# Sparse attention's best keys: the first query block takes out its 16 least keys in two rounds, not its 112 best in 14

## The chip, the cores and the metric

The kernel runs on one core of a Trainium2 chip, in one launch. The metric is the device time in microseconds (us). The core has five engines that each work through their own instructions in the order of the program: TensorE (PE in the profile, with PEld for its weight loads), VectorE (DVE), ScalarE (ACT), GpSimd (POOL) and SyncE (SP), which here only starts transfers from memory. Work tiles have 128 partitions.

## The reference, cut to what matters

The program is a decoder trunk of two layers over 528 tokens (16 learned meta tokens, then 512 real ones), width 1024, in float32. Layer 0 is differential attention, layer 1 is sparse attention in which a small indexer picks the keys of each query; a gated feed-forward network (FFN) with a short convolution stands behind each. What is changed lies in the indexer of layer 1:

```python
topk = min(TOPK_MAX, n_keys // 4)            # 128
score = einsum('bqhk,bqh->bqk', relu(raw), wb)
causal = k_pos[None, :] <= q_pos[:, None]
score = where(causal & (k_pos < N_META)[None, :], BIG_SCORE, score)
score = where(causal, score, -inf)
top_val, top_idx = lax.top_k(score, topk)
valid = top_val > -inf
ks = gather(k, top_idx); vs = gather(v, top_idx)
s = where(valid, einsum(qb, ks), -inf)       # softmax over the picked keys
```

The 16 meta tokens are always among the 128 picked, so each query picks 112 of the others. Masked keys never count, whether picked or not.

## The kernel before

**Tiling.** Everything is held transposed, features on the partitions and tokens on the free axis. Queries are handled in one block of the 16 meta tokens (block 0) and four blocks of 128 (blocks 1 to 4, `BLK`, L38); block b sees 16 + 128 b keys. Block 1 therefore has 144 keys, 128 of them not meta.

**Arithmetic.** A float32 product is made of three rounded ones. `two` (L394) splits a tensor into a high part (a copy on ScalarE, `wh` for a weight slab of 128x1024) and a low part (a subtraction, `wl`), and `project` (L454) multiplies 48 times for each slab: high by high, high by low, low by high, over 8 pieces and two token spans. There are two pairs of `wh` and `wl`, so the next slab is split while one is in use.

**Layer 1.** `index_task` (L1070) gives eight passes of indexer scores that are summed into `acc[b]`, one tile for each block. `topk_task` (L1099) then marks the best keys of its block: 14 rounds, each of which finds the eight greatest values of the 128 rows (`max`) and overwrites them with `TAKEN` (`match_replace`, which the profile shows as a MATCH_VALUE_LOAD and a MATCH_REPLACE8). At the end a `tensor_scalar` turns marked places into 0 and all others into -1e30, a `tensor_tensor` lays the causal mask over it, GpSimd clears the meta columns, and `acc[b]` is the bias of all 16 heads. A head (L1186) may start once block 2's bias is there; its parts wait for their own block's (`e_bias`). Meanwhile PE works through the projections of q, k and v ("filler"). q and k of a pair of heads go through `rope` (multiply by `Cr`, shuffle, multiply by `Sr`, add), are split into `X` and `K` tiles (`q_stack`, `k_stack`), and each `K` is completed by a transfer from one half of its partitions to the other, issued by GpSimd. Only then can PE make the head's scores; the softmax is a fused subtract-and-minimum on VectorE (an ISA or CUSTOM_DVE instruction) and an exponential on ScalarE, and `probs_T` transposes and splits the result (`ph`, `pl`).

**What sets the order.** Nothing is ordered by hand. `Plan.run` (L292) holds all tasks and emits, again and again, the instruction that can start first by a table of costs (`_cost`, L71), with ties of up to 30 ns going to the task of higher priority. Work that VectorE or GpSimd could do alike stands in an `Alt` (L115), and the planner takes the engine on which it would end first, with a surcharge on VectorE (`plan.bias`). So when one instruction of a task goes or comes, the order behind it on all engines is drawn anew. The order, once drawn, is fixed in the program; at run time each engine waits for semaphores. All planned instructions have the line L272.

Of the kernel before, what the change touches and what calls it, by code (L numbers as in the profile page):

```python
# [13 lines left out]
ALU = mybir.AluOpType  # L14
# [6 lines left out]
NMETA = 16  # L21
# [7 lines left out]
NEG = -1e30  # L29
TAKEN = -3e38  # L30
TOPK = 128

BLK = [(0, 16)] + [(16 + 128 * i, 144 + 128 * i) for i in range(4)]
# [291 lines left out]
def hybrid_trunk(ctx: ExitStack, tc: tile.TileContext, A, out):  # L325
    nc = tc.nc
    plan = Plan(tc)
    v, s, g, pe, sy = (Engine(n, e) for n, e in (
        ("dve", nc.vector), ("act", nc.scalar), ("pool", nc.gpsimd), ("pe", nc.tensor), ("sp", nc.sync)))
# [8 lines left out]
    def bufs(name, n, shape, dtype=F32):  # L338
        return Buf([sb(f"{name}{i}", shape, dtype) for i in range(n)])
# [9 lines left out]
    TT = bufs("tt", 10, [P, T + 2])  # L349
# [642 lines left out]
    def attention1(norm, nxt):  # L992
# [106 lines left out]
        def topk_task(b):  # L1099
            yield e_acc[b]  # L1100
            st = yield STAT
            m8 = st[:, :8]
            w = acc[b][:, NMETA:]

            for _ in range((TOPK - NMETA) // 8):
                yield v.max(out=m8, in_=w)
                yield v.match_replace(out=w, in_to_replace=m8, in_values=w, imm_value=TAKEN)
            yield v.tensor_scalar(out=w, in0=w, scalar1=TAKEN, scalar2=NEG, op0=ALU.not_equal, op1=ALU.mult)
            if b == 4:
                plan.bias = SPARE_TAKEN  # L1110
            w = acc[b][:, BLK[b][0]:]
            yield v.tensor_tensor(out=w, in0=w, in1=mask[:, T - P:], op=ALU.min)
            yield g.memset(acc[b][:, :NMETA], 0.0)
            STAT.put(st)
            e_bias[b].set()
# [147 lines left out]
        for b in range(1, 5):  # L1263
            spawn(topk_task(b), 4)
# [193 lines left out]
```

## Time and profile before

| what | value |
|---|---|
| median of 3 runs | 1422.75 us (1421.95 to 1424.04) |
| the profiled execution, its own time | 1423.88 us |
| its span, first to last instruction | 1422.0 us |
| PE busy | 1367.0 us, 96% |
| VectorE busy | 953.3 us, 67% |
| ScalarE busy | 678.9 us, 48% |
| GpSimd busy | 333.7 us, 23% |
| VectorE, `max` and `match_replace` of all four blocks, first to last start | 744.1 to 804.3 us |
| granted clock of PE, mean | 0.989 |

A row of a timeline gives start, duration, engine, operation, and what was written from what (buffer numbers left out, so `acc` is any block's); in brackets the idle time before it and what ended it. A row of the windows gives for a stretch the busy time of each engine and its number of instructions, the share of full clock that PE was granted, and the load of the transfer engines. Durations of neighbours on VectorE overlap by some 0.06 us; from start to start counts.

### The profile page before, as it was taken

To read this page: it belongs to the slowest core of one execution; us is meant where nothing else is said; L and a number is where in the kernel's file an instruction comes from. 1 tells how busy PE (TensorE), PEld (TensorE's weight loads), DVE (VectorE), ACT (ScalarE), POOL (GpSimd) and SP (SyncE) were. 2 spreads that over 40 slices of the span, in tenths; PEclk is the share of its full clock that TensorE was granted. 3 is DMA by queue.
4 is the path that set the end of the run, shared out by engine and by line. 5 is a ranking of instruction groups with operands and counts; after the bars stand their busy time and mean duration, and the time that the engine had idled before them with its cause. 6 is when DMAs were issued, how large, how long until landed. Compare 5 with 4: busy or idle time off the path is not lost.

```text
span 1422.0 us, 26126 instructions
## 1 busy us (share of the span) xinstructions
PE 1367.0 (96%) x10662; PEld 1328.6 (93%) x10662; DVE 953.3 (67%) x1613; ACT 678.9 (48%) x1224; POOL 333.7 (23%) x432
## 2 busy tenths in 40 slices
PE   8899999999999999999989979999999999999997
PEld 7899998899999999999989879998999989989997
DVE  6976775457645754775699978887667637646764
ACT  5576665444423432443365376777444424423454
POOL 4645655420000000000347543332210000000012
PEclk9999999999999999999999989999999999999999
DMA  5323223223233223332212322232223232233333
GB/s 191 102 61 81 71 75 90 72 78 99 84 90 100 85 83 102 89 90 69 90 45 75 90 62 60 68 78 65 89 90 89 90 104 89 93 99 92 91 115 107
DMA packets 36519, 124.30 MB, mean 87 GB/s; under 512 B 4400, under 2 KB 4784, under 8 KB 36400
## 3 DMA queue, kind: packets, MB, share of 16 engines
q1 hardware_dynamic: 32544, 111.84, 25.9%
q0 software_dynamic: 2560, 8.65, 2.9%
q8 instruction: 84, 1.38, 0.4%
q10 hardware_dynamic: 1296, 2.15, 0.4%
q14 instruction: 35, 0.29, 0.1%
HBM read 111.88 MB, written 2.10 MB: 80 GB/s over the span
## 4 chain that ended last, share of the span: by engine, by line
PE 68%; DVE 10%; ACT 2%; issue 1%; POOL 0%; POOLq 0%; ACTq 0%; DVEq 0%
PE ps L272 68%; DVE tt L272 3%; DVE acc L272 3%; DVE st L272 2%; DVE wl L272 1%; DVE ns L272 1%; ACT ns L272 0%; ACT wh L272 0%; ACT tt L272 0%; DVE K L272 0%; POOL tt L272 0%; DVE pl L272 0%; ACT K L272 0%; DVE X L272 0%; ACT ph L272 0%
## 5 line engine op out<-in xcount | busy, mean ns | idle before, releaser
L272 PE MATMUL ps<-R,wh 128*128 128x256 f32 (+4 forms) x4000 | 679.4, 290 | 6.4 <-ACT wh L272 2.2
L272 PEld LDWEIGHTS ps<-R,wh 128*128 128x128 f32 (+1 forms) x4000 | 561.8, 190 | 15.2 <-ACT wh L272 2.4
L272 PE MATMUL ps<-R,K 128*128 128x272 f32 (+3 forms) x3264 | 430.6, 290 | 0.0
L272 PE MATMUL ps<-R,wl 128*128 128x272 f32 (+3 forms) x2000 | 423.1, 289 | 3.5 <-DVE wl L272 3.5
L272 PEld LDWEIGHTS ps<-R,K 128*128 128x128 f32 x3264 | 412.5, 189 | 8.4
L272 PEld LDWEIGHTS ps<-R,wl 128*128 128x128 f32 x2000 | 312.2, 189 | 7.3 <-DVE wl L272 4.4
L272 ACT CAST wh<-raw 128x1024 fp32r<-128x1024 f32 (+1 forms) x134 | 138.6, 1034 | 171.7 <-PE ps L272 127.0
L272 DVE TENSOR_TENSOR wl<-raw,wh 128x1024 fp32r<-128x1024 f32 (+1 forms) x124 | 156.5, 1262 | 23.1 <-ACT wh L272 21.7
L272 ACT CAST K<-raw 128x1024 fp32r<-128x1024 f32 (+1 forms) x77 | 79.1, 1027 | 140.0 <-PE ps L272 125.7
L272 DVE TENSOR_TENSOR h<-ps,h 128x528 f32<-128x528 f32 (+3 forms) x70 | 45.7, 653 | 143.1 <-PE ps L272 143.1
L272 POOL TENSOR_TENSOR acc<-acc,tt 128x528 f32<-128x528 f32 (+1 forms) x26 | 43.3, 1667 | 415.1 <-ACT tt L272 411.9
L272 DVE TENSOR_TENSOR tt<-ps,rbc 128x528 f32<-128x528 f32 (+2 forms) x89 | 62.4, 701 | 114.5 <-PE ps L272 110.1
L272 DVE SCALAR_TENSOR_TENSOR tt<-tt,cw,tt 128x528 f32<-128x528 f32 (+1 forms) x176 | 133.4, 758 | 8.2 <-ACT tt L272 4.9
L272 ACT CAST R<-tt 128x512 fp32r<-128x512 f32 (+2 forms) x84 | 48.7, 586 | 155.4 <-DVE tt L272 155.0
L272 DVE TENSOR_TENSOR K<-raw,K 128x1024 fp32r<-128x1024 f32 (+1 forms) x76 | 91.4, 1203 | 13.6 <-ACT K L272 12.3
L272 PE MATMUL ps<-K,X 128*128 128x272 f32 (+2 forms) x464 | 79.9, 308 | 13.2 <-DVE st L272 6.9
L272 ACT ACTIVATE ns<-ns,st 128x528 f32<-128x528 f32 (+4 forms) x160 | 82.1, 514 | 20.1 <-DVE st L272 17.1
L272 PEld LDWEIGHTS ps<-K,X 128*128 128x128 f32 x464 | 66.4, 184 | 18.0 <-DVE st L272 8.2
L272 ACT ACTIVATE tt<-tt,cw 128x528 f32<-128x528 f32 (+1 forms) x88 | 72.4, 822 | 14.6 <-DVE tt L272 14.5
L272 POOL MEMSET tt<- 128x2 f32 x44 | 4.2, 100 | 302.0 <-DVE tt L272 302.0
L272 POOL TENSOR_TENSOR tt<-tt,Sr 128x528 f32<-128x528 f32 x29 | 44.9, 1549 | 115.7 <-DVE tt L272 115.7
L272 ACT ACTIVATE tt<-tt 128x528 f32<-128x528 f32 (+1 forms) x44 | 28.1, 639 | 81.4 <-DVE tt L272 81.4
(112 smaller groups left out, 1315.5 us busy)
## 6 DMA issues: line engine op xcount, KB each, us to landing
raw<-in_ffn_up_dram SPq DMA_DIRECT2D x88, 512.0 KB, 3.6
raw<-in_ffn_down_dram SPq DMA_DIRECT2D x32, 448.0 KB, 3.3
raw<-in_da_qkv_dram SPq DMA_DIRECT2D x24, 512.0 KB, 3.7
raw<-in_dsa_qkv_dram SPq DMA_DIRECT2D x24, 512.0 KB, 3.6
raw<-in_ffn_down_dram SPq DMA_DIRECT2D x22, 512.0 KB, 3.6
K<-K POOLq DMA_DIRECT2D x32, 264.0 KB, 3.1
raw<-in_da_o_dram SPq DMA_DIRECT2D x8, 512.0 KB, 3.7
raw<-in_dsa_o_dram SPq DMA_DIRECT2D x8, 512.0 KB, 3.7
```

Source lines behind the costliest of these rows:

```text
L272: self.tc.keep_in_program_order(op.call(*op.a, **op.k))
```

## The change

Only `topk_task` is changed, and in it only what block 1 does, the one block with no more than `TOPK` (128) keys beside the meta ones. Instead of marking 112 of its 128 keys it marks the 16 others. ScalarE writes the negated scores, in reversed order, into a borrowed tile of the pool `TT`; two rounds of `max` and `match_replace` mark the 16 greatest of them, so the 16 least scores; and the `tensor_scalar` reads the tile backwards and gives the marked places -1e30 and the others 0. The reversal keeps the pick among equal scores as it was. Blocks 2, 3 and 4 keep their 14 rounds.

```diff
@@ topk_task
             w = acc[b][:, NMETA:]
-
-            for _ in range((TOPK - NMETA) // 8):
-                yield v.max(out=m8, in_=w)
-                yield v.match_replace(out=w, in_to_replace=m8, in_values=w, imm_value=TAKEN)
-            yield v.tensor_scalar(out=w, in0=w, scalar1=TAKEN, scalar2=NEG, op0=ALU.not_equal, op1=ALU.mult)
+            n = BLK[b][1] - NMETA
+            if n <= TOPK:
+                t = yield TT
+                u = t[:, :n]
+                yield s.mul(u, w[:, ::-1], -1.0)
+                for _ in range((n - (TOPK - NMETA)) // 8):
+                    yield v.max(out=m8, in_=u)
+                    yield v.match_replace(out=u, in_to_replace=m8, in_values=u, imm_value=TAKEN)
+                yield v.tensor_scalar(out=w, in0=u[:, ::-1], scalar1=TAKEN, scalar2=NEG, op0=ALU.is_equal, op1=ALU.mult)
+                TT.put(t)
+            else:
+                for _ in range((TOPK - NMETA) // 8):
+                    ...
```

The planner draws a new order from there to the end of layer 1's attention; the order in front of it and that of the second FFN are the same. Over the whole program VectorE has 32 rows fewer (24 of the rounds, and 8 net that go to GpSimd: 5 K splits, 4 X splits and 3 additions, against which 2 `wl` splits and 2 others come back), GpSimd 8 more, PE as many as before.

On VectorE, at the end of block 1's two rounds (`acc_142` is block 1's tile, `acc_143` block 2's, `tt_104` the borrowed one):

```order
+L272 TENSOR_SCALAR acc_142<-tt_104 128x128
 L272 MAX st_136<-acc_143 128x8
-L272 MAX st_135<-acc_142 128x8
+L272 TENSOR_TENSOR acc_142<-acc_142,mask 128x128
 L272 MATCH_REPLACE acc_143<-st_136,acc_143 128x256
-L272 MATCH_REPLACE acc_142<-st_135,acc_142 128x128
+L272 TENSOR_TENSOR wl_115<-raw_111,wh_114 128x1024
 L272 MAX st_136<-acc_143 128x8
-L272 MAX st_135<-acc_142 128x8
+L272 TENSOR_TENSOR tt_109<-tt_108,Cr 128x528
```

Block 1's rounds are gone from between those of block 2, and a weight split and the rotation of q stand in their place.

On GpSimd, at the same time of the program (`R_75`, `R_69` are parts of v; `X_118` and `K_123` belong to the first pair of heads):

```order
 L272 TENSOR_TENSOR R_75<-tt_107,R_75 128x4x64
 L272 TENSOR_TENSOR R_69<-tt_107,R_69 128x4x64
-L272 TENSOR_TENSOR wl_115<-raw_111,wh_114 128x1024
-L272 TENSOR_TENSOR wl_117<-raw_112,wh_116 128x1024
+L272 TENSOR_TENSOR tt_101<-tt_101,Sr 128x528
+L272 TENSOR_TENSOR tt_109<-tt_109,tt_101 128x528
+L272 TENSOR_TENSOR X_118<-tt_109,X_118 64x528
+L272 TENSOR_TENSOR tt_106<-tt_106,Sr 128x528
+L272 TENSOR_TENSOR tt_103<-tt_103,tt_106 128x528
+L272 TENSOR_TENSOR K_123<-tt_103,K_123 64x528
+L272 DMA K_123<-K_123 64x1056
```

Two weight splits leave GpSimd, and the rotation of the first pair of heads is done there from end to end.

On PE, 12 rows ahead of the end of a projection (`R`, `wl`, `wh` are a projection, `K_123,X_118` the first head's scores):

```order
 L272 MATMUL ps_154<-R_72,wl_115 128x272
 L272 MATMUL ps_154<-R_72,wl_115 128x256
+L272 MATMUL ps_153<-K_123,X_118 128x272 x2
+L272 MATMUL ps_153<-K_123,X_118 128x256 x2
+L272 MATMUL ps_152<-K_123,X_118 128x400 x2
+L272 MATMUL ps_152<-K_123,X_118 128x272 x2
+L272 MATMUL ps_151<-K_123,X_118 128x256 x2
+L272 MATMUL ps_151<-K_123,X_118 16x256 x2
 L272 MATMUL ps_154<-R_80,wh_114 128x272
 L272 MATMUL ps_154<-R_80,wh_114 128x256
```

The first head's scores stand 42 rows further ahead than before, inside one projection and not in the middle of the next.

More of the change, by code (lines that the diff above doesn't have):

```diff
@@ L1103, in topk_task @@
             w = acc[b][:, NMETA:]
-            for _ in range((TOPK - NMETA) // 8):
-                yield v.max(out=m8, in_=w)
-                yield v.match_replace(out=w, in_to_replace=m8, in_values=w, imm_value=TAKEN)
-            yield v.tensor_scalar(out=w, in0=w, scalar1=TAKEN, scalar2=NEG, op0=ALU.not_equal, op1=ALU.mult)
+            n = BLK[b][1] - NMETA
[10 more added lines that the diff above has]
+                for _ in range((TOPK - NMETA) // 8):
+                    yield v.max(out=m8, in_=w)
+                    yield v.match_replace(out=w, in_to_replace=m8, in_values=w, imm_value=TAKEN)
+                yield v.tensor_scalar(out=w, in0=w, scalar1=TAKEN, scalar2=NEG, op0=ALU.not_equal, op1=ALU.mult)
             if b == 4:
```

## The prediction

> **What bounds the kernel now.** I read first the windows of ten microseconds around the top-k, to see which engine is full there and what PE does:
>
> ```profile
> core 0: us, PE busy (x) PEld busy (x) DVE busy (x) ACT busy (x) POOL busy (x), PEclk, DMA share, GB/s
> 730.00:740.00 10.00, 7.00 (x53) 6.61 (x54) 10.00 (x16) 5.86 (x14) 4.72 (x3) 1.00 0.01 2
> 780.00:790.00 10.00, 10.00 (x85) 10.00 (x83) 10.00 (x44) 3.82 (x10) 7.51 (x10) 1.00 0.21 61
> 790.00:800.00 10.00, 10.00 (x83) 10.00 (x83) 10.00 (x50) 3.10 (x4) 2.46 (x2) 1.00 0.35 105
> 800.00:810.00 10.00, 8.64 (x69) 8.21 (x67) 9.96 (x16) 4.96 (x7) 6.80 (x5) 1.00 0.17 54
> 810.00:820.00 10.00, 6.00 (x44) 5.53 (x44) 9.77 (x12) 3.51 (x7) 6.92 (x6) 1.00 0.60 156
> 820.00:830.00 10.00, 7.98 (x39) 7.57 (x39) 8.45 (x26) 7.61 (x19) 4.21 (x7) 0.66 0.28 59
> 830.00:840.00 10.00, 5.44 (x28) 4.94 (x29) 8.65 (x21) 6.58 (x19) 6.70 (x7) 0.71 0.28 73
> ```
>
> VectorE is full up to 820. PE hides that until 800, because it has projections to do; then it runs dry, and from 820 it also runs at a lower clock. PE's own timeline says how long it stood:
>
> ```profile
> 808.05 0.65 PE L272 MATMUL ps<-R,wh 128*128 128x272 f32 x4
> 811.04 0.51 PE L272 MATMUL ps<-R,wl 128*128 128x272 f32 x2 [2.33 <-DVE wl L272]
> ...
> 814.31 1.26 PE L272 MATMUL ps<-K,X 128*128 128x272 f32 x8
> 816.61 0.74 PE L272 MATMUL ps<-K,X 128*128 128x256 f32 x4 [1.04 <-ACT tt L272]
> ...
> 821.30 1.25 PE L272 MATMUL ps<-K,X 128*128 128x272 f32 x4 [3.22 <-DVE st L272]
> ...
> 832.86 1.09 PE L272 MATMUL ps<-ident,ns 128*128 128x128 f32 x8 [3.58 <-DVE pl L272]
> 835.65 1.22 PE L272 MATMUL ps<-K,X 128*128 128x256 f32 x4 [1.70 <-DVE st L272]
> 836.68 1.08 PE L272 MATMUL ps<-R,wh 128*128 128x272 f32 x4
> ```
>
> Five waits, 11.9 us in all, four of them on VectorE. The clock costs more on top: 7.98 us busy at 0.66 and 5.44 us at 0.71 are, at full clock, 2.7 and 1.6 us less. So 16.2 us are to be had at most here, and only here: what VectorE saves elsewhere lies under a busy PE.
>
> **What is taken away.** VectorE's timeline in the same stretch:
>
> ```profile
> 782.90 1.20 DVE L272 TENSOR_TENSOR wl<-raw,wh 128x1024 fp32r<-128x1024 f32 x1
> ...
> 784.42 0.34 DVE L272 SCALAR_TENSOR_TENSOR acc<-ns,wi,acc 128x128 f32<-128x128 f32 x1
> ...
> 788.20 0.60 DVE L272 MAX8 st<-acc 128x8 f32<-128x256 f32 x2
> 788.73 0.07 DVE L272 MATCH_VALUE_LOAD acc<-st,acc 128x8 f32 x1
> 788.79 0.40 DVE L272 MATCH_REPLACE8 acc<-st,acc 128x256 f32<-128x256 f32 x1
> 789.12 0.07 DVE L272 MATCH_VALUE_LOAD acc<-st,acc 128x8 f32 x1
> 789.18 0.27 DVE L272 MATCH_REPLACE8 acc<-st,acc 128x128 f32<-128x128 f32 x1
> 789.38 0.60 DVE L272 MAX8 st<-acc 128x8 f32<-128x256 f32 x2
> ...
> 798.45 0.70 DVE L272 TENSOR_TENSOR tt<-tt,Cr 128x528 f32<-128x528 f32 x1
> 799.07 0.29 DVE L272 MAX8 st<-acc 128x8 f32<-128x128 f32 x1
> ...
> 800.19 2.33 DVE L272 TENSOR_TENSOR wl<-raw,wh 128x1024 fp32r<-128x1024 f32 x1
> ...
> 806.38 0.28 DVE L272 TENSOR_TENSOR acc<-acc,mask 128x128 f32<-128x128 f32 x1
> ...
> 808.66 2.33 DVE L272 TENSOR_TENSOR wl<-raw,wh 128x1024 fp32r<-128x1024 f32 x1
> ...
> 820.55 0.69 DVE L272 CUSTOM_DVE_ANT_0 ns<-ps,acc 128x528 f32<-128x528 f32 x1
> ```
>
> Block 1's scores are complete at 784.8, its bias at 806.7; the first softmax instruction comes at 820.55. A round of block 1 between two of block 2 takes 0.2 us of `max` (0.60 less the 0.40 of 256 elements), 0.06 of the value load and 0.20 of the replace (789.18 to 789.38), 0.46 us. Twelve rounds are **5.5 us** (busy, by the durations, 12 times 0.27 + 0.07 + 0.27 = 7.3). Block 1's bias itself is not what a head waits for, since it needs block 2's first.
>
> **What is added and moved.** On ScalarE one 128x128 multiplication, about 0.3 us (the trace has none that reads backwards; below by nothing, above by the 0.6 of a 528-wide copy; I take 0.3). It stands ahead of v's last small copies and of a weight cast, and waits for 784.8:
>
> ```profile
> 784.19 1.05 ACT L272 CAST wh<-raw 128x1024 fp32r<-128x1024 f32 x1 [1.73 <-PE ps L272]
> ...
> 790.03 1.05 ACT L272 CAST wh<-raw 128x1024 fp32r<-128x1024 f32 x1 [3.69 <-PE ps L272]
> ```
>
> The copies queued between take 0.7 us (785.2 to 785.9), so that cast starts at 785.9, 1.7 us late. (The second row shows when PE ends a projection and frees its slab, 790.0.) On GpSimd and its transfers:
>
> ```profile
> 787.59 2.41 POOL L272 TENSOR_TENSOR wl<-raw,wh 128x1024 fp32r<-128x1024 f32 x1
> 791.16 2.41 POOL L272 TENSOR_TENSOR wl<-raw,wh 128x1024 fp32r<-128x1024 f32 x1 [1.16 <-ACT wh L272]
> ...
> 800.12 1.32 POOL L272 TENSOR_TENSOR tt<-tt,Sr 128x528 f32<-128x528 f32 x1 [6.50 <-DVE tt L272]
> ...
> 808.03 1.87 POOL L272 TENSOR_TENSOR K<-tt,K 64x528 fp32r<-64x528 f32 x1 [2.09 <-ACT K L272]
> ```
>
> ```profile
> K<-K POOLq DMA_DIRECT2D x6, 264.0 KB, 3.0
> ```
>
> The two `wl` come back to VectorE, 1.2 us each where GpSimd is still. Where GpSimd subtracts or multiplies meanwhile, the same instruction takes 2.33 us (800.19 beside 800.12, 808.66 beside 808.03): 1.1 us is waiting. GpSimd's `wl` at 787.59 and 791.16 lay beside `max` rounds that stayed at their length, and paid nothing. So in the new order I let a two-input VectorE instruction and one of GpSimd follow each other. The Trainium skill says the same in "SBUF — State Buffer", section "SBUF: two separate sides": the shared port pair is an exclusive lock. It also says that whoever starts first keeps it; by that alone the third split below could lose its turn as well, and the sum would be 1.3 us less of a gain.
>
> **The new stretch, step by step**, in the order drawn for each engine, with 0.62 us for a 528-wide VectorE step (798.45 to 799.07), 1.32 for one on GpSimd, 0.46 for a free round of block 2, 1.18 for a pair of rounds (788.20 to 789.38), 1.2 for a `wl`:
> - Block 1's two rounds and bias lie among four of block 2: VectorE 784.7 to 788.95. Then the `wl` that GpSimd made; GpSimd's work on v is late by the 1.7 us and holds it until 789.6: done 790.8. PE wants it 0.5 us after it starts the next projection at 790.0 (it ran without a gap before): stall 0.4.
> - q's rotation, four rounds, the second `wl` behind GpSimd's addition: done 796.8. PE stall 0.2.
> - k's rotation, X split, four rounds: 802.05; the third `wl` done 803.35. PE stall 0.5.
> - Block 2 ends at 807.6. GpSimd's chain for the first K: shuffle done 800.75, multiply 802.15, addition behind the `wl` 804.65, cast 805.3, split 806.7, transfer 807.0 and 3.0 us more: 810.1. PE arrives at these scores at 807.6 (12 rows, 1.5 us, ahead of the slab that began at 808.05, plus the stalls): **stall 2.5**, in place of the 2.33.
> - The other half of that pair: transfer 811.5, PE there at 812.45. The next slab's `wl` is ready at 810.05, PE needs it at 814.8: no stall, where now 2.33 are.
> - VectorE has the second pair's steps done at 813.9: the first softmax instruction at **813.9 instead of 820.55**. Both heads' 17.8, exponentials in step; transposes at 819.3 find them ready. The next K is through GpSimd (818.3) and transfer at 821.7, PE at 821.1: stall 0.6.
> - `pl` of the first head needs ScalarE's `ph` (824.7, behind the second head's exponentials): 825.7. PE stands for that buffer from 823.7: stall 2.1, where 3.58 were.
>
> PE then has exactly the matrix work done that it had before at 836.68 (one projection, the second one complete, three heads' scores, one head's transposes), at 826.9. Stalls 6.3 us; 16.2 less 6.3 is **9.9 us**, if the clock stays up. VectorE reaches the same place (the second `pl`) about as much earlier, so PE isn't merely running ahead into the next wait.
>
> Behind it, up to 1000, the order is drawn anew as well, and I did not follow it piece by piece. I allow 2 us for worse waits: as bounds 1.6 us gained (all that PE idles from 850 to 950 now, by the windows below) and 6 lost.
>
> ```profile
> 850.00:900.00 50.00, 49.47 (x386) 46.94 (x384) 40.07 (x91) 35.87 (x82) 16.37 (x19) 1.00 0.19 54
> 900.00:950.00 50.00, 48.92 (x389) 47.26 (x388) 41.96 (x93) 35.21 (x83) 21.22 (x27) 1.00 0.34 86
> ```
>
> That leaves 7.9. The profiled execution took 1423.88 (span 1422.0 and 1.9 around it): 1416.0. The median of the runs shown is 1.1 lower, so **1414.9 us**.
>
> **The rivals.**
> (a) *The clock falls anyway.* In the trace it fell after the wait of 3.22 us; in 730 to 740, with 3.0 us idle in shorter pieces, and after the 2.33 us at 808, it held. My longest wait is 2.5, uncertain by 1, and a second follows. If it falls: 4.3 us back, **1419.2**. The Trainium skill ("TensorE: Matmul & The Clock Gate", "Why this matters for your kernels") puts the limit at gaps over about 3 us, which the trace fits; the case hangs on my 2.5 being right.
> (b) *The lead is given back.* From 850 on VectorE is 80 to 84% busy and ScalarE 70%; if the new order lets PE run ahead of them, it waits out at the end what it gained: **1422.5**. Against it: the eight instructions that move to GpSimd relieve VectorE just there, and GpSimd has 16 to 21 of 50 us.
> (c) *Slower: GpSimd becomes the bound of the K chain.* The chain that ended last shows where layer 1's attention ends:
>
> ```profile
> 997.55 395.26 PE ps L272 x2956
> ```
>
> Five more K splits and four X splits lie on it, 1.3 to 1.9 us each against 0.62, and a K needs multiply, addition, split and 3.0 us of transfer in series there. Eight pairs of heads pass PE from 814.3 until its last long run begins, some 23 us each; GpSimd's part of a pair is about 9, so it decides only where the planner puts scores within 3 us of their transfer, as at 810.1. If four of the seven pairs stall there for 3 us and the clock falls once, that is 16.3 against 9.9: 6.4 slower than the profile, **1429**.
> (d) *It doesn't do what it says*, for instance since a backward read is slow: at 1 us more on two instructions, 1 to 2 us less gain; that lies inside the range.
>
> **How the numbers follow.** Forecast 0.53, (a) 0.24, (b) 0.13, (c) 0.10. A change of 0.2% (2.8 us) is about what a measurement of this kernel tells from none. Forecast and (a) lie beyond it, but for a small part of (a); (b) is the same: faster 0.76, same 0.13, slower 0.11. The range goes from 1409.5 (no later waits and only half the stalls: 16.2 less 3.2) to 1422.0, into (b); the forecast's own range is 1410 to 1418.
>
> **What would show it.** Right: the first softmax instruction on VectorE near 814 instead of 820.55; PE idle from 800 to 850 at 5 to 7 us instead of 11.9; PE's clock at 1.00 there; the second FFN begins some 8 us earlier, and beyond it nothing differs. Wrong: a wait of over 3 us on a K transfer with clock 0.6 behind it (a); idle PE between 850 and 990 above 8 us (b, c); `wl` on VectorE at 2.3 us each with PE waiting behind every one.

## The result, and the profile after

| what | before, same chip | after |
|---|---|---|
| median of 4 runs each | 1422.49 us (1421.95 to 1424.04) | 1413.42 us (1413.02 to 1414.18) |
| ratio, 95% interval | | 0.9933 (0.9922 to 0.9945) |
| the profiled execution, its own time | 1423.88 us | 1413.13 us |
| its span | 1422.0 us | 1411.2 us |

The change is 9.1 us faster; 1414.9 was forecast, with a range from 1409.5 to 1422.0. The difference is well beyond 0.2%, so "faster" was the right side. The profiled execution shows where it lies. The chain of waits after ends in the same piece as before, of the same length, 10.8 us earlier (before: 997.55):

```profile
986.73 395.26 PE ps L272 x2956
```

So the whole difference arose ahead of it. PE's timeline after, its waits between 800 and 850, of which the bracket gives length and releaser:

```profile
803.42 0.52 PE L272 MATMUL ps<-R,wl 128*128 128x272 f32 x2 [0.41 <-DVE wl L272]
...
810.05 2.39 PE L272 MATMUL ps<-K,X 128*128 128x272 f32 x12 [2.45 <-DMA K<-K]
...
814.86 2.21 PE L272 MATMUL ps<-K,X 128*128 128x272 f32 x12 [1.09 <-DVE st L272]
...
826.28 0.88 PE L272 MATMUL ps<-K,X 128*128 128x400 f32 x4 [0.49 <-DVE pl L272]
...
828.64 0.74 PE L272 MATMUL ps<-K,X 128*128 128x256 f32 x4 [1.48 <-DVE st L272]
```

The waits are 5.9 us in all, where 11.9 were. The wait for `pl` (3.58 before) is 0.49 now; the longest is for the first head's `K`. VectorE's timeline after, at the places that the prediction dated:

```profile
787.98 0.60 DVE L272 TENSOR_SCALAR acc<-tt 128x128 f32<-128x128 f32 x1
...
789.67 1.21 DVE L272 TENSOR_TENSOR wl<-raw,wh 128x1024 fp32r<-128x1024 f32 x1
...
794.63 2.16 DVE L272 TENSOR_TENSOR wl<-raw,wh 128x1024 fp32r<-128x1024 f32 x1
...
802.07 1.29 DVE L272 TENSOR_TENSOR wl<-raw,wh 128x1024 fp32r<-128x1024 f32 x1
...
814.10 0.70 DVE L272 CUSTOM_DVE_ANT_0 ns<-ps,acc 128x528 f32<-128x528 f32 x1
```

The first row is the one that reads backwards, the last is the first softmax instruction. The windows of the stretch, first of before and then of after (columns as in the prediction's windows), give one number for each kernel:

```profile
800.00:850.00 50.00, 38.06 (x254) 35.91 (x253) 42.63 (x89) 29.27 (x67) 26.54 (x30) 0.86 0.30 76
```

```profile
800.00:850.00 50.00, 43.97 (x328) 41.22 (x327) 43.39 (x107) 33.46 (x76) 26.57 (x32) 0.97 0.34 86
```

PE idles 50 less its busy time, 11.9 us before and 6.0 after, and loses its busy time times what its clock is below 1: 38.06 times 0.14 is 5.3 us before, 43.97 times 0.03 is 1.3 after. Together **17.3 us before and 7.4 after**; the 9.9 between them is nearly all of the gain. I call this sum the loss of the stretch and use it for every kernel below.

### The profile page after: what moved, and what is told of

Same layout as the page of the kernel before. It is cut to its first block, busy times and chain, and to the rows that moved or that the text cites. A ratio compares the mean times of both kernels' runs of the same rounds, so it can differ in the third digit from the quotient of the medians.

```text
span 1411.2 us, 26101 instructions
## 1 busy us (share of the span) xinstructions
PE 1364.9 (97%) x10662; PEld 1326.9 (94%) x10662; DVE 941.0 (67%) x1569; ACT 677.8 (48%) x1225; POOL 338.7 (24%) x440
## 4 chain that ended last, share of the span: by engine, by line
PE 69%; DVE 9%; issue 2%; ACT 1%; POOL 0%; POOLq 0%; ACTq 0%; DVEq 0%
PE ps L272 69%; DVE acc L272 3%; DVE tt L272 2%; DVE st L272 2%; DVE wl L272 1%; DVE ns L272 0%; DVE pl L272 0%; ACT tt L272 0%; ACT K L272 0%; DVE X L272 0%; ACT ns L272 0%; ACT wh L272 0%; ACT ph L272 0%; ACT X L272 0%; DVE K L272 0%
```

## The experiments

The result left two readings. By the first, mine, VectorE has less to do and PE therefore waits less. By the second, the planner merely drew a better order, and would have with the rounds in place. The old order can be kept row for row while rounds are left out, and the new one kept while rounds are put back.

**1 and 2. The old order with rounds left out.** The planner still counts all 14 rounds of block 1, but those from the third on (or from the ninth on) are not issued, so that block 1 has only its first 16 (or 64) keys marked.

```diff
 def _emit(self, op):
-    self.tc.keep_in_program_order(op.call(*op.a, **op.k))
+    getattr(op, 'ghost', False) or self.tc.keep_in_program_order(op.call(*op.a, **op.k))
 topk_task:
+    o.ghost = b in (1,) and i >= 2      # 12 rounds; i >= 8 leaves out 6
```

> The order of before on all engines, row for row, with block 1's last 12 rounds left out on VectorE and nothing put in their place (so block 1's bias marks 16 keys as best and not 112; no negation, no borrowed tile, no move between VectorE and GpSimd). If VectorE's time in its full stretch is the cause, the 5.5 us taken out there pull the softmax forward: first softmax instruction near 815 instead of 820.55, PE idle from 800 to 850 at 4 to 8 us instead of 11.9, time 1412 to 1417. If the newly drawn order is the cause (weight splits back on VectorE, the first K on GpSimd, scores earlier on PE), the old order keeps its waits: 1420 to 1423.

> As the old order with rounds out, but only 6 of block 1's 14 rounds left out (its bias marks 64 keys as best). If VectorE's time there sets the end, half the rounds give about half of what 12 give: 1416.5 to 1419.5. If the order is the cause: 1421 to 1423. If it works by a threshold (the clock, one wait), either all of it or nothing.

Measured: with 12 rounds out 1420.53 us (1418.81 to 1422.73) beside 1423.06 of the kernel before, ratio 0.9984 (0.9974 to 0.9993); with 6 out 1422.03 (1419.53 to 1422.96), ratio 0.9993 (0.9983 to 1.0002), which can't be told from no change. Twelve rounds are worth 2.5 us in the old order, not 5.5, and not 9. VectorE's timeline of the 12-out kernel shows why:

```profile
786.53 0.41 DVE L272 MAX8 st<-acc 128x8 f32<-128x256 f32 x1
786.97 0.09 DVE L272 MATCH_VALUE_LOAD acc<-st,acc 128x8 f32 x1
787.05 0.41 DVE L272 MATCH_REPLACE8 acc<-st,acc 128x256 f32<-128x256 f32 x1
787.50 0.43 DVE L272 MAX8 st<-acc 128x8 f32<-128x256 f32 x1
...
795.38 0.29 DVE L272 TENSOR_SCALAR acc<-acc 128x256 f32<-128x256 f32 x1
...
797.20 1.20 DVE L272 TENSOR_TENSOR wl<-raw,wh 128x1024 fp32r<-128x1024 f32 x1
...
801.97 0.28 DVE L272 TENSOR_TENSOR acc<-acc,mask 128x128 f32<-128x128 f32 x1
802.17 1.82 DVE L272 TENSOR_TENSOR tt<-tt,tt 128x528 f32<-128x528 f32 x1
...
817.29 0.69 DVE L272 CUSTOM_DVE_ANT_0 ns<-ps,acc 128x528 f32<-128x528 f32 x1
```

The same places in the kernel before:

```profile
787.03 0.61 DVE L272 MAX8 st<-acc 128x8 f32<-128x256 f32 x2
...
797.59 0.29 DVE L272 TENSOR_SCALAR acc<-acc 128x256 f32<-128x256 f32 x1
...
806.58 0.69 DVE L272 TENSOR_TENSOR tt<-tt,tt 128x528 f32<-128x528 f32 x1
```

- Nine rounds of block 2, alone, take 8.85 us (786.53 to 795.38), 0.98 each; with a round of block 1 in every one they took 10.56 (787.03 to 797.59), 1.17 each. Nine of block 1's rounds were worth **0.19 us each**, 1.7 in all. A `max` and the `match_replace` behind it wait for each other: without the other block's instructions between them, each starts only when the one before has ended in full (786.53 and 0.41 make 786.94, the next starts at 786.97), while in before neighbours overlap. Block 1's rounds largely lay in that wait.
- From there to block 1's mask 2.2 us are saved (797.59 to 806.38 before, 795.38 to 801.97 here). Three rounds of block 1 that stood alone among other work are 1.4 of it, some 0.46 each; the rest is mostly the `wl` at 797.20. Before, GpSimd began its multiplication first (800.12 against 800.19) and `wl` took 2.33; here VectorE begins first (GpSimd at 797.38) and it takes 1.20.
- From the mask to the first softmax instruction 1.15 are given back (14.17 us before, 15.32 here): now it is the addition at 802.17 that takes 1.82 where it took 0.69.

Together 2.75 us, and the first softmax instruction is 3.26 earlier, since this execution was 0.5 ahead at block 1's last score. PE's waits in this kernel:

```profile
818.05 1.25 PE L272 MATMUL ps<-K,X 128*128 128x272 f32 x4 [3.21 <-DVE st L272]
...
829.61 1.97 PE L272 MATMUL ps<-ident,ns 128*128 128x128 f32 x8 [3.83 <-DVE pl L272]
```

The long ones, 3.22 and 3.58 in before, are still there, and half clock follows each of them, as it did there. The windows of this kernel:

```profile
818.00:820.00 2.00, 1.95 (x9) 1.95 (x10) 1.94 (x10) 1.45 (x4) 0.95 (x4) 0.50 0.66 135
832.00:834.00 2.00, 1.60 (x7) 1.47 (x8) 2.00 (x10) 1.55 (x6) 0.96 (x1) 0.50 0.00 0
800.00:850.00 50.00, 40.61 (x282) 38.00 (x281) 42.07 (x94) 32.90 (x79) 24.39 (x29) 0.86 0.30 74
```

The loss of the stretch is 9.4 us idle and 5.7 by the clock, 15.1 where before has 17.3.

**3. The new order with the rounds put back.** The change, with 24 rows of dummy rounds on a free tile, one behind each of VectorE's next instructions; the result is the change's.

```diff
 def _emit(self, op):
     self.tc.keep_in_program_order(op.call(*op.a, **op.k))
+    if op.eng == "dve" and self.extra:
+        self.tc.keep_in_program_order(self.extra.pop(0)())
 topk_task, block 1:
+    for _ in range(12):
+        plan.extra.append(lambda: nc.vector.max(out=xt[:, 128:136], in_=xt[:, :128]))
+        plan.extra.append(lambda: nc.vector.match_replace(out=xt[:, :128], ...))
```

> The order of the change on all engines, with 12 rounds of the size of block 1's put back on VectorE, one instruction behind each of the next 24 there, on a tile that nobody waits for (the result is unchanged). If VectorE's time is the cause, 5.5 us more in the full stretch push the splits and the softmax back: first softmax near 819 to 820, time 1418.5 to 1423. If the new order is the cause, the time stays at 1412.5 to 1415.

Measured: 1416.03 us (1415.58 to 1416.93), ratio 0.9949 (0.9935 to 0.9964). With the same number of rounds on VectorE as before, 7.0 of the 9 us remain. The first softmax instruction and the longest wait, from VectorE's and PE's timelines:

```profile
816.33 0.70 DVE L272 CUSTOM_DVE_ANT_0 ns<-ps,acc 128x528 f32<-128x528 f32 x1
```

```profile
817.10 3.22 PE L272 MATMUL ps<-K,X 128*128 128x272 f32 x12 [3.00 <-DVE st L272]
```

The softmax is 2.2 us later than in the change, but still 4.2 earlier than before, and the wait for `pl`, 3.58 before and the second to halve the clock, is gone. Half clock still comes twice, behind the 3.00 and behind a wait for a weight split, by PE's timeline and the window of the stretch:

```profile
806.09 0.79 PE L272 MATMUL ps<-R,wl 128*128 128x272 f32 x2 [2.68 <-DVE wl L272]
```

```profile
800.00:850.00 50.00, 43.45 (x309) 41.49 (x307) 42.73 (x110) 30.43 (x69) 24.02 (x30) 0.90 0.33 88
```

The loss of the stretch is 6.6 us idle and 4.3 by the clock, 10.9 where the change has 7.4 and before has 17.3. The rounds cost about 2 us in this order too (0.9949 against 0.9933 of the change is 2.3 us, against 0.9937 of its repeat below 1.7), and the order is the larger part. That spoke for the second reading, but the order of the change is one that the planner drew for fewer rounds. It could still be that only fewer rounds allow such an order.

**4. The first K on VectorE.** This tests rival (c) at the one place where it shows, the 2.45 us for the first `K`: the addition and the split that GpSimd makes for it go to VectorE, at the same place of the order.

```diff
+    here = on_vector if (m, c) == (0, 1) else lambda x: x    # GpSimd's add and subtract as nc.vector.tensor_tensor
-    t = yield from rope(raw[:, :T], Cr, Sr, lambda: TT.put(raw))
-    yield from stacks(t, c, to)
+    t = yield from here(rope(raw[:, :T], Cr, Sr, lambda: TT.put(raw)))
+    yield from here(stacks(t, c, to))
```

> The order of the change; of the first K alone the addition and the split run on VectorE, at their place in the order, and not on GpSimd (result unchanged). PE's longest wait, 2.45 us for that K's transfer, is then for a chain shorter by some 1.5 us (0.7 each instead of 2.17 and 1.34). If GpSimd's chain sets that wait and the wait sets the end: PE's wait 0.8 to 1.6, time 1411.5 to 1412.8. If VectorE is still what ends last, its 1.4 us more are paid: the wait shrinks, the next one grows, 1413 to 1415.

Measured: 1414.31 us (1413.28 to 1414.96), ratio 0.9936 (0.9921 to 0.9951), the change's own time. PE's timeline:

```profile
809.56 1.96 PE L272 MATMUL ps<-K,X 128*128 128x272 f32 x12 [1.80 <-POOL st L272]
...
815.02 3.13 PE L272 MATMUL ps<-K,X 128*128 128x272 f32 x12 [2.18 <-DVE st L272]
```

The wait on the transfer gives way to one of 1.80, and the next wait, for VectorE's softmax, grows from 1.09 to 2.18. What was taken from one wait went to the next: the softmax itself (814.26 us, for 814.10) came no earlier, so PE only waited at another place. Since the two instructions also load VectorE, this doesn't show what a faster transfer would be worth for nothing. Nor did the chain become the expected 1.5 us shorter: in GpSimd's timeline the transfer is issued at 806.38, where the change has 806.91. So it shows only that 0.5 us less in the chain of the first `K` gains nothing: PE's next wait ends with VectorE's softmax in both kernels, and half clock takes 3.1 us here and 1.3 in the change.

**5 to 8. Other draws of the order.** The planner's surcharge on VectorE in layer 1's attention is one number (800 ns, `SPARE`). At 700 or 1000 it draws other orders, for the old kernel with all 14 rounds and for the change alike.

```diff
-    plan.bias = SPARE
+    plan.bias = 700.0      # or 1000.0
```

> The kernel before with 14 rounds, and one number of the planner changed: the surcharge on VectorE in layer 1's attention is 700 and not 800, so the order is drawn anew from there on for a reason that has nothing to do with the rounds. If the order that came with the change was a lucky draw (some 7 of the 9 us), another draw moves the old kernel as well, by 2 us or more to either side, 1412 to 1430. If the old kernel's time is set by its rounds, it stays at 1421 to 1425.

> The changed kernel with the surcharge at 700. If fewer rounds give the planner a better order by their nature, this stands 7 to 11 us below the old kernel at the same surcharge. If only the 2.5 us of the rounds themselves are safe and the rest is the draw, the difference of the two at 700 is anything from 8 us slower to 12 us faster.

> The kernel before with the surcharge at 1000: a third draw of its order. Lucky draw: 1412 to 1430 and not the time of the other two by more than 2 us. Set by the rounds: 1421 to 1425.

> The changed kernel with the surcharge at 1000. By their nature better: 7 to 11 us below the old kernel at 1000, and 1412 to 1416. Lucky draw: its distance to the old kernel at 1000 differs from 9 us by more than 3 us.

Measured, beside 1423.43 of the kernel before:

| surcharge | old kernel, all rounds: median us | the change: median us | difference |
|---|---|---|---|
| 800 | 1422.49 | 1413.42 | 9.1 us |
| 700 | 1415.48 (1413.36 to 1418.36), ratio 0.9939 (0.9923 to 0.9954) | 1412.75 (1411.76 to 1413.53), ratio 0.9918 (0.9896 to 0.9941) | 2.7 us |
| 1000 | 1417.03 (1415.67 to 1418.11), ratio 0.9952 (0.9933 to 0.9972) | 1412.29 (two runs: 1412.26, 1412.32), ratio 0.9924 (0.9895 to 0.9952) | 4.7 us |

(The first row is from the runs of the result; its two kernels ran beside each other. In each of the other two rows the intervals of the two kernels overlap, so that 2.7 and 4.7 are rough.) The old kernel, with nothing taken from its top-k, gains 6.4 to 8.0 us by another surcharge. So the better order doesn't need fewer rounds, and the second reading holds for the larger part. The first softmax instruction of the old kernel at 1000:

```profile
814.17 0.70 DVE L272 CUSTOM_DVE_ANT_0 ns<-ps,acc 128x528 f32<-128x528 f32 x1
```

That is where the change has it (814.10), with all rounds in place. But an early softmax is not what makes an order fast. In the old kernel at 700 (the repeat below, 7 us faster than before) it comes later than before's 820.55:

```profile
822.24 0.71 DVE L272 CUSTOM_DVE_ANT_0 ns<-ps,acc 128x528 f32<-128x528 f32 x1
```

Of three draws of the old kernel, the one at 800 was the slow one.

**9 to 12. The rounds in a third order, and repeats.** The old kernel at 700 once more; the same order with 12 rounds left out as in the first experiment; the change and the change at 1000 once more, all four on one chip.

> The old kernel with all 14 rounds, surcharge 700, once more, beside the next kernel: 1414 to 1417.

> The order of the old kernel at surcharge 700, row for row, with block 1's last 12 rounds left out on VectorE (its bias marks 16 keys as best). If the rounds are worth the same in any order (2.5 us in the old one, about 2 to 3 in the new one), this is 1.5 to 3.5 us below the kernel beside it. If in this order PE's work covers them: within 1 us of it. If they set the whole stretch: 5 us or more below.

> The change as it is, once more, beside the others: 1412.5 to 1414.5, that is 8 to 10 us below the kernel before on this chip and 1 to 4 below the old kernel with surcharge 700.

> The change with surcharge 1000, beside the change as it is. If its lower single figure (1412.29) was the draw of its order and not of the run, 0.7 to 2 us below the change; if it was noise, within 0.5 us of it.

| kernel | median us (lowest to highest) | ratio (95% interval) |
|---|---|---|
| before | 1423.0 | |
| old kernel at 700 | 1416.05 (1415.78 to 1416.55) | 0.9947 (0.9930 to 0.9964) |
| the same order, 12 rounds out | 1413.83 (1413.10 to 1416.32) | 0.9935 (0.9920 to 0.9950) |
| the change | 1414.59 (1413.67 to 1415.54) | 0.9937 (0.9923 to 0.9952) |
| the change at 1000 | 1412.19 (1411.24 to 1413.19) | 0.9921 (0.9906 to 0.9935) |

Twelve rounds are worth 2.2 us in this third order, in which all other rows stay as they are. The intervals of the two overlap, as those of the new order with and without the rounds do, so a single figure is near what can be measured; but three orders gave 2.5, some 2, and 2.2. The change at a surcharge of 1000 is the fastest of all: 2.4 us under the change beside it, their runs don't overlap, their intervals do. Its window of the stretch, and that of the old kernel at 700:

```profile
800.00:850.00 50.00, 45.77 (x343) 43.38 (x343) 43.15 (x101) 35.12 (x82) 26.90 (x33) 0.97 0.34 86
```

```profile
800.00:850.00 50.00, 41.45 (x310) 39.88 (x309) 46.40 (x109) 31.60 (x73) 25.38 (x28) 0.93 0.33 86
```

| kernel | idle | lost by the clock | loss of the stretch | median less the kernel before beside it |
|---|---|---|---|---|
| before | 11.9 | 5.3 | 17.3 | 0 |
| old order, 6 rounds out | 10.1 | 5.6 | 15.7 | -1.0 |
| old order, 12 rounds out | 9.4 | 5.7 | 15.1 | -2.5 |
| old kernel at 700 | 8.6 | 2.9 | 11.5 | -7.0 |
| new order, 12 rounds back | 6.6 | 4.3 | 10.9 | -7.0 |
| the change at 700 | 6.6 | 3.0 | 9.6 | -10.7 |
| the change, first K on VectorE | 5.8 | 3.1 | 8.9 | -8.8 |
| old kernel at 1000 | 7.2 | 1.3 | 8.5 | -6.4 |
| old kernel at 700, 12 rounds out | 6.9 | 1.3 | 8.2 | -9.2 |
| the change | 6.0 | 1.3 | 7.4 | -9.1 |
| the change at 1000 | 4.2 | 1.4 | 5.6 | -10.8 |

Each loss is of one profiled execution. Two rows don't fit: by their loss the change at 700 should gain 7.7 us and gains 10.7, and the old kernel at 1000 should gain 8.8 and gains 6.4. PE's idle time from 850 to 1000 is a part of both (1.0 us less than before in the one, 1.3 more in the other); the rest is open. In the other eight the time follows the loss of this one stretch to 1.2 us; of the repeats that are not in the table, the first run of the old kernel at 700 is 2.1 off and the second of the change 1.6.

What stays open is which part of a new order carries the gain. Three parts come to mind in the change: that the first head's scores stand further ahead on PE, that weight splits come back to VectorE, and that block 2's rounds are spread among other work. These were not tried apart, but none of them is needed. In the old kernel at 700 the first head's scores begin at 816.96, later than before (814.31). In GpSimd's timeline three weight splits lie between 780 and 830, where before has two (787.59 and 791.16):

```profile
787.00 2.39 POOL L272 TENSOR_TENSOR wl<-raw,wh 128x1024 fp32r<-128x1024 f32 x1
791.73 2.40 POOL L272 TENSOR_TENSOR wl<-raw,wh 128x1024 fp32r<-128x1024 f32 x1 [2.33 <-ACT wh L272]
797.75 2.60 POOL L272 TENSOR_TENSOR wl<-raw,wh 128x1024 fp32r<-128x1024 f32 x1 [3.56 <-ACT wh L272]
```

And on VectorE block 2's rounds alternate with block 1's as before and end at the same time (before: 797.59):

```profile
797.41 0.28 DVE L272 TENSOR_SCALAR acc<-acc 128x256 f32<-128x256 f32 x1
```

It is 7 us faster all the same, with two longer waits than the change has, by PE's timeline,

```profile
816.96 1.82 PE L272 MATMUL ps<-K,X 128*128 128x272 f32 x12 [3.34 <-DMA K<-K]
...
823.87 2.37 PE L272 MATMUL ps<-K,X 128*128 128x272 f32 x8 [4.36 <-DVE st L272]
```

which make 7.7 of its 8.6 us of idle time, where before has five waits and 11.9, and half clock comes once, where before has it twice.

## Why the prediction was right, and where it was wrong

- **What bounds the kernel: right.** Only the stretch behind 800 had something to give, and 9.9 of the 10.8 us of the profiled execution come from it.
- **The new stretch, step by step: right on VectorE and for the first `K`; PE's waits right in the sum only.** `wl` splits done at 790.8, 796.8, 803.35 were forecast; they ended at 790.9, 796.8, 803.4. The first softmax instruction came at 814.10 (813.9), the wait on the first `K` was 2.45 at 810.05 (2.5 at 810.1), PE's idle time 6.0 (5 to 7), the waits 5.9 in all (6.3). But apart from the first `K` these are not the waits that were forecast: those on `wl` came to 0.41 instead of 1.1, the one on `pl` to 0.49 instead of 2.1, the 0.6 on the next `K` did not come, and PE waited 1.09 and 1.48 for `st`, where nothing was forecast. Some 2.9 us too much and 2.6 too little cancel, so that the sum fits is luck. Nor do the listed costs give the listed times: four rounds at 0.46 and three steps of 0.62 lead from 796.8 to 800.5, not to 802.05. Two instructions that meet were put one behind the other, and did so: in GpSimd's timeline,

```profile
794.38 1.32 POOL L272 TENSOR_TENSOR tt<-tt,tt 128x528 f32<-128x528 f32 x1
...
802.36 2.17 POOL L272 TENSOR_TENSOR tt<-tt,tt 128x528 f32<-128x528 f32 x1
```

  the addition at 794.38 was first, and VectorE's `wl` at 794.63 took 2.16 instead of 1.2; at 802.07 VectorE was first, kept its 1.29, and GpSimd's addition took 2.17. Whoever began first kept its length, as the Trainium skill says in "SBUF — State Buffer", section "SBUF: two separate sides"; the loss of the third split's turn, which I had weighed by it, did not come about, since VectorE began 0.3 us before.
- **"Twelve rounds are 5.5 us": wrong.** It priced a round of block 1 by what it occupies between two others, 0.46 us. Nine of the twelve stood in the wait of block 2's rounds for their own results, and taking them out gives 0.19 each; three stood alone and give some 0.46 by their rows. That is 3.1 us on VectorE and 2.5 at the end. (The step-by-step list also gives 0.46 for a free round of block 2. By the prediction's own rows that one takes 0.72, the pair's 1.18 less the 0.46.) The sum did not rest on the 5.5, since it was made from the waits in the new order. But it left the cause wrong: I told the 9.9 us as what VectorE's relief is worth, when the relief is worth 2 to 2.5 and the other 6 to 7 come from a new draw.
- **"If the clock stays up": partly wrong.** It fell behind the 2.45 us, by this row of the change's windows of 2 us, to half:

```profile
812.00:814.00 2.00, 1.77 (x9) 1.42 (x6) 1.95 (x4) 0.00 (x0) 0.00 (x0) 0.50 0.52 213
```

  At 814 to 816 it was back at 0.89 and then at 1.00, so that this cost 1.3 us and not the 4.3 of rival (a), which took before's two falls for its measure. That the stretch gave 9.9 us, just what was forecast, is luck here too: the clock cost before 5.3 in the whole stretch and not the 4.3 read from 820 to 840, and it cost the change 1.3 where nothing was put down.
- **The 2 us allowed for worse waits behind 850: not needed.** The windows of before and then of after say that PE idled 5.6 us from 850 to 1000 and idles 4.3 now:

```profile
850.00:1000.00 150.00, 144.42 (x1122) 136.74 (x1121) 118.72 (x264) 106.12 (x245) 47.47 (x68) 1.00 0.24 65
```

```profile
850.00:1000.00 150.00, 145.73 (x1143) 139.03 (x1142) 114.05 (x249) 106.81 (x244) 56.94 (x76) 1.00 0.25 65
```

  So rival (b), the lead given back, did not come, and it is this allowance by which the forecast fell short: 9.9 for the stretch and 1.3 from here are 11.2, where 7.9 was written down and the profiled executions differ by 10.8. The medians differ by 9.1, so the step from one profiled execution to the median is worth as much as the miss of 1.5 us itself.
- **Rivals (c) and (d).** The K chain on GpSimd bound PE at the one place that was named, for 2.45 us, and taking its addition and split off GpSimd, which made it 0.5 us shorter, gained nothing; nowhere did it make the kernel slower. The instruction that reads backwards takes 0.60 us on VectorE and the negation 0.31 on ScalarE; (d) falls. The 0.60 is not the price of the direction: in the change at 700, with GpSimd idle beside it, the same instruction takes 0.21.

```profile
789.62 0.21 DVE L272 TENSOR_SCALAR acc<-tt 128x128 f32<-128x128 f32 x1
```

## What to carry to other kernels

When a planner draws the order anew, a change is timed together with a draw: before crediting it, keep the old order and leave the work out, keep the new order and put it back, and draw the old kernel's order again by another cost. Here that split 9.1 us into some 2 to 2.5 for the rounds and 6 to 7 for the draw, and gave a version below both. And price a removed instruction by what starts earlier without it, not by its own length: one that stands in another's wait gives back only what exceeds that wait.

## What the runs showed that was not expected

The clock does not fall at one length of wait. In before it held after 2.33 us (811.04); the change fell after 2.45. In the old kernel at 700 it held after 3.34 (816.96), by its windows of 2 us:

```profile
816.00:818.00 2.00, 1.04 (x7) 1.07 (x8) 1.97 (x3) 1.10 (x2) 1.25 (x2) 1.00 0.31 63
818.00:820.00 2.00, 1.51 (x13) 1.25 (x11) 2.00 (x2) 0.00 (x0) 1.55 (x2) 1.00 0.92 173
```

At one place in front of the changed stretch both kernels have the same program and the same wait, in PE's timeline of before and then of after,

```profile
732.25 0.96 PE L272 MATMUL ps<-K,X 128*128 128x272 f32 x6 [2.28 <-DVE tt L272]
```

```profile
732.07 1.27 PE L272 MATMUL ps<-K,X 128*128 128x272 f32 x6 [2.28 <-DVE tt L272]
```

and the clock of the ten microseconds around them is 1.00 in the first (in the prediction's windows) and 0.83 in the second:

```profile
730.00:740.00 10.00, 7.93 (x52) 7.93 (x53) 10.00 (x16) 5.48 (x13) 4.73 (x3) 0.83 0.00 1
```

VectorE is full there, and it cost nothing: the split that starts at 782.90 before starts at 782.96 after. The Trainium skill ("TensorE: Matmul & The Clock Gate", "Part 1: The HAM clock gate") calls the gate's activity window free-running, and says that for this reason the number of slow matmuls at a kernel's start varies from run to run. The pair of rows fits that; no run here shows the window itself. The limit of about 3 us that the prediction took from the page did not hold here: half clock followed a wait of 2.45 us and did not follow one of 3.34.
